# Attention with two heads' scores in the two row halves of TensorE, a pinned order around it, and a readout in two steps

## The chip, the cores and the metric

The kernel runs on one core of one Trainium2 chip. Its engines work in parallel, each through its own list in order: TensorE (PE in the profile; PEld is its weight loads), VectorE (DVE), ScalarE (ACT), GpSimd (POOL) and SyncE (SP, which issues loads). The metric is the device time of one execution in microseconds (us); lower is better. Of several executions the median is taken.

## The reference

Two layers of a hybrid backbone over 512 latent tokens and 256 context tokens of width 1024. Layer 0 is the even mixer: one input projection feeds a gated linear attention (GLA, 4 heads) and a softmax attention with 8 query heads in 2 groups of 64-wide keys and values; both results are concatenated, projected, normalised and added; then a feed-forward layer. Layer 1 is a different recurrence (HGRN2) and another feed-forward layer. What matters here is the attention of layer 0:

```python
def _softmax_attend(q, k, v):
    s = jnp.einsum('bhgqd,bhkd->bhgqk', q, k, preferred_element_type=jnp.float32) * (ATT_HEAD_DIM ** -0.5)
    p = jax.nn.softmax(s, axis=-1).astype(v.dtype)
    return jnp.einsum('bhgqk,bhkd->bhgqd', p, v)
...
    o_lat = jnp.concatenate([a_lat, b_lat], axis=-1)
...
    b_ctx = _softmax_attend(qa[:, :, :, :n_ctx], ka[:, :, :n_ctx], va[:, :, :n_ctx])
```

Latent queries read all 768 keys, context queries only the 256 context keys. The GLA half is read out as `_gated_readout`: a root-mean-square norm of each head times a gate.

## The kernel before

Tokens are handled in six tiles of 128: 0 to 3 latent, 4 and 5 context. Values that need more than one float32r pass are kept as two parts, H (the rounded value) and L (the remainder), and a product is summed from several passes.

**Attention** (class `Attention`). `keys` (L154) transposes keys into `pk` and writes H and L. A head is 64 wide, so each group's keys fill half of the rows; GpSimd copies them into the other half (L165), for both groups. `queries` (L167) transposes a tile's queries; for each head H lies in one half of the rows and L in the other. `scores` (L179) then needs two passes of all 128 rows a head, keys H and keys L, which sum all four products. It fills one `mm` tile (1024 columns, two PSUM banks; there are two such tiles), VectorE takes the row minimum (L196; the keys carry the factor −0.125), ScalarE the Exp with its row sum (L198), VectorE the reciprocal (L199). `turned` (L201) transposes the 768 probabilities in six blocks through two small PSUM tiles and copies them out on ScalarE (the first four) and VectorE (the other two, L210). `values` (L212) multiplies values by transposed probabilities, both groups at once in the two column halves of TensorE, into `po` (attO in the profile). `rows` (L230; rB) spreads the reciprocals, `done` (L248) multiplies them on (L252) and splits the result into H and L of `cat`, the input of the output projection (L665, L666).

`context` (L255) does tiles 4 and 5, four heads to a tile of scores; `latent` (L304) does tiles 0 to 3 one head a step, 32 heads in all: scores of head i, transposes of head i − 3, a part of the values of the four heads before that. PSUM has eight banks: two `mm` tiles of two, `sc0` and `sc1` of one, two `tr` of one.

**What sets the order.** `even_mixer` (L1068) holds generators under short names and runs them by hand-written lists: `x` is a step of the context's attention, `y` of the latent attention, `r1` a tile of the GLA readout (`readout`, L1174: square, sum, rstd, then two multiplies, L1180 to L1186), `t` a piece of `gated_T` (L1270; transposes of the GLA output into `cat`, catT), `M` a step of `mod_group` (L507; loads of eight 512 KB blocks, then 32 small matmuls, then two transposes), `g1` a part of the GLA gates. After the first `y x y g1` the list is

```python
            run("x y x y M x y x")
            behind = {6: "t", 7: "r1", 9: "t", 10: "r1", 14: "M", 15: "r1", 16: "M", 17: "t", 19: "t", 22: "t", 24: "t", 26: "t", 29: "t"}
            for i in range(3, 32 + 7):
                run("y " + behind.get(i, ""))
```

While `self.pinned` is set, `mm` and `tr` (L370, L373) keep all matmuls and transposes in the order in which the program issues them. Instructions of ScalarE and VectorE are not pinned: the scheduler of the framework orders them by its own estimate of when they can start. What follows, `out_proj` (L1523), is not pinned either, so that its matmuls can move forward between those of attention. It loads eight units of 128 rows of `even_w_out`; `unit` (L688) loads a block on SP into one of three `raw` tiles and splits it into H on ScalarE (L699) and L on VectorE (L700).

Of the kernel before, what the change touches and what calls it, by code (L numbers as in the profile page):

```python
# [133 lines left out]
class Attention:  # L134
# [10 lines left out]
    def __init__(self, net, natq, natk, cat):  # L145
        self.net, self.nc, self.natq, self.natk, self.cat = net, net.nc, natq, natk, cat
        self.q, self.k, self.po, self.r, self.o, self.ended = {}, {}, {}, {}, {}, []

    def other(self):

        t = list(self.po)[-1]
        return t % 2 if t in self.ended else 1 - t % 2

    def keys(self, g, gn, HL):  # L154

        nc, net, half = self.nc, self.net, self.half
        pk = net.tr_tile("kT")[:, : gn * P]
        for i in range(gn):
            net.tr(pk[:, i * P : (i + 1) * P], self.natk[:, g + i, 0:128], net.ident)
        for n in range(2):  # L160
            H, L = (x[half[n], n, :] for x in HL)
            nc.scalar.mul(H, pk[half[n]], -0.125)
            nc.vector.scalar_tensor_tensor(L, pk[half[n]], -0.125, H.bitcast(F32), op0=ALU.mult, op1=ALU.subtract)
            for x in HL:
                nc.gpsimd.tensor_copy(x[half[1 - n], n, :], x[half[n], n, :].bitcast(F32))  # L165

    def queries(self, t, q):  # L167
        nc, net, half = self.nc, self.net, self.half
# [4 lines left out]
        for n in range(2):  # L173
            H = q[half[n], 4 * n : 4 * n + 4, :]
            nc.scalar.copy(H, pv[half[n]])
            nc.vector.tensor_tensor(q[half[1 - n], 4 * n : 4 * n + 4, :], pv[half[n]], H.bitcast(F32), op=ALU.subtract)
        self.q[t] = q

    def scores(self, t, heads, p):  # L179

        nc, net = self.nc, self.net
        s = net.mm_tile("S")
        nk = p.shape[-1]
        w = 1024 // len(heads)
        for x, hd in enumerate(heads):
            at = w * x
            for ks in self.k[int(t >= LT)]:
                m = ks[0].shape[-1]
                for i, k in enumerate(ks):
                    net.mm(s[:, at : at + m], self.q[t][:, hd, :], k[:, hd // 4, :], start=(i == 0), stop=(i == 1))  # L190
                at += m
        sv = s.rearrange("p (x k) -> p x k", k=w)[:, :, :nk]
        mx, sm = (net.sm.tile([P, len(heads)], F32, tag=tag, name=tag) for tag in (("amx", "asm") if len(heads) == 1 else ("ms4", "ss4")))
        if t not in self.r:
            self.r[t] = net.sm.tile([P, 8], F32, tag="ars", name="ars")
        nc.vector.tensor_reduce(mx, sv, axis=AX.X, op=ALU.min)  # L196
        for x in range(len(heads)):
            nc.scalar.activation(p[:, x, :], sv[:, x, :], AF.Exp, bias=mx[:, x : x + 1], scale=-1.0, accum_out=sm[:, x : x + 1])  # L198
        nc.vector.reciprocal(self.r[t][:, heads[0] : heads[0] + len(heads)], sm)  # L199

    def turned(self, p, dsts, vector, scratch=False):  # L201

        nc, net = self.nc, self.net
        for b, dst in enumerate(dsts):
            m = dst.shape[1]
            pt = net.sc_tile("pT", self.other()) if b and scratch else net.tr_tile("pT")
# [3 lines left out]
            (nc.vector.tensor_copy if b in vector else nc.scalar.copy)(dst, src)  # L210
# [19 lines left out]
    def rows(self, t):  # L230
# [14 lines left out]
        nc.scalar.copy(w[:, :512], pr)  # L245
        self.o[t] = w[:, :512], w[:, 512:]

    def done(self, t):  # L248
        nc, net = self.nc, self.net
        self.ended.append(t)  # L250
        rb, o = self.o.pop(t)
        nc.vector.tensor_tensor(o, self.po[t], rb, op=ALU.mult)  # L252
        net.put(self.cat, slice(4, 8), slice(t * P, (t + 1) * P), o.rearrange("p (j i) -> p j i", j=4))

    def context(self):  # L255
        wp = self.net.wp
        wide = lambda tag, name, dt=F32R: wp.tile([P, WU], dt, tag=tag, bufs=4, name=name)
        kc = wide("wH", "kc").rearrange("p (x n i) -> p x n i", x=2, n=2)
        self.k[1] = [(kc[:, 0], kc[:, 1])]
        ps, pTs = {}, {}  # L260

        def queries(t, tag):
            self.queries(t, wide(tag, f"qs{t}").rearrange("p (h i) -> p h i", h=8))

        def scores(b):
            ps[b] = wp.tile([P, WU], F32, tag="raw", bufs=3, name=f"prob{b}")
            self.scores(LT + b // 2, range(4 * (b % 2), 4 * (b % 2) + 4), ps[b].rearrange("p (x k) -> p x k", x=4))
# [6 lines left out]
        def values(t):  # L274
            self.rows(LT + t)
            self.values(LT + t, 0, lambda n, ci: pTs[2 * t + n][:, :, ci, :])
# [27 lines left out]
    def latent(self, ap):  # L304
        kl = [ap.tile([P, 2, SEQ], F32R, name=f"k{x}") for x in "HL"]
        self.k[0] = [kl] + self.k[1]
        q = lambda t: ap.tile([P, 8, P], F32R, tag="qs", bufs=2, name=f"qs{t}")
# [5 lines left out]
        ahead = 3  # L313
        heads = (0, 4, 1, 5, 2, 6, 3, 7)
        ps, pTs = {}, {}
        for i in range(8 * LT + ahead + 4):
            t, at = divmod(i, 8)
            if t < LT:
                ps[i] = ap.tile([P, NT], F32, tag="prob", bufs=4, name="prob")
                self.scores(t, (heads[at],), ps[i][:, None, :])  # L320
            j = i - ahead
            if 0 <= j < 8 * LT:
                if j % 4 == 0:
                    pTs[j // 4] = ap.tile([P, 2, NTT, 2, P], F32, tag="probT", bufs=2, name="probT")
                to = pTs[j // 4][:, j % 2, :, j % 4 // 2, :]
                self.turned(ps.pop(j), (to[:, :4], to[:, 4:]), (1,), True)
            if 4 <= j:
                t0, x = divmod(j // 4 - 1, 2)
                pT = pTs[j // 4 - 1]
                self.values(t0, 2 * x, lambda n, ci: pT[:, n, ci], (slice(0, 1), slice(1, 3), slice(3, 4), slice(4, 6))[j % 4])  # L330
                if x and j % 4 == 2:
                    self.rows(t0)
                if x and j % 4 == 3:
                    self.done(t0)
            if t + 1 < LT and at == 4:
                self.queries(t + 1, q(t + 1))
# [3 lines left out]
class Net:  # L340
# [3 lines left out]
    def __init__(self, ctx, tc, I, out):  # L344
        self.tc, self.nc, self.I, self.out = tc, tc.nc, I, out
        tc.nc.scalar.preload_act_table_set("silu_and_others")
        self.side = 0
        self.whole = False
# [339 lines left out]
    def unit(self, src, k, n, pool=None, to=None):  # L688
# [10 lines left out]
        nc.scalar.copy(H[:, :m], raw[:, :m])  # L699
        nc.vector.tensor_tensor(L[:, :m], raw[:, :m], H[:, :m].bitcast(F32), op=ALU.subtract)  # L700
        return H[:, :m].rearrange("p (k n) -> p k n", k=k), L[:, :m].rearrange("p (k n) -> p k n", k=k)
# [189 lines left out]
    def rows_unit(self, w, c, pool=None, paired=False):  # L891
# [5 lines left out]
        return self.unit(src, 1, D, pool)  # L897
# [170 lines left out]
    def even_mixer(self, h, mix, zu, last):  # L1068
# [105 lines left out]
        def readout(c, tiles=tiles):  # L1174

            for t0 in tiles:
# [3 lines left out]
                nc.scalar.activation(sq.rearrange("p (t n) -> p t n", t=2), gv[:, t0 : t0 + 2, cs], AF.Square)  # L1180
                ss = self.sm.tile([P, 4], F32, tag="ss4", name="ss4")
                nc.vector.tensor_reduce(ss, sq.rearrange("p (x v) -> p x v", v=P), axis=AX.X, op=ALU.add)
                rs = self.rstd(ss, P, 4, 4.0 if c else 1.0)
                rb = rs.rearrange("p (t h) -> p t h", t=2)[:, :, :, None].to_broadcast([P, 2, 2, P])
# [706 lines left out]
```

## Time and profile before

| | |
|---|---|
| median of three runs | 1740.32 us |
| lowest, highest | 1738.23, 1741.54 us |
| the profiled execution's own time | 1738.56 us |
| its span, first to last instruction | 1736.4 us |
| granted TensorE clock, mean | 0.996 |
| latent attention, first scores to last values | 259.9 to 354.0 us of the span |

The span is the part of an execution that the profile covers. Lines L... are lines of the kernel's file; since all matmuls go through two helpers, TensorE's rows are told apart by the tiles: S is scores, pT transposed probabilities, attO values, rB reciprocals, qT and kT query and key transposes, catT the GLA output, mod_acc the modulation. A row such as `out<-in engine op shape x6` merges neighbours of one kind. Matmuls are pipelined, so a row's length holds its latency too; the pace is read from starts. What stands in brackets is idle time of the engine ahead of the row and who ended it; "issue" means nobody that the profile shows. Where a float32 matmul (not float32r) is one instruction in the program, the trace has two.

### The profile page before, as it was taken

How to read it: one execution, taken by the hardware profiler on the slowest of the kernel's cores; microseconds unless marked ns; L12 is line 12 of the kernel's file. 1: busy time of each engine (PE TensorE's matmuls, PEld its weight loads, DVE VectorE, ACT ScalarE, POOL GpSimd, SP SyncE). 2: the span in 40 equal slices, each digit the busy share in tenths (PEclk: the TensorE clock that was granted, in tenths of full speed). 3: DMA queues.
4: the chain of work that ended last, by engine and by line, in shares of the span. 5: the costliest groups of instructions: out<-in, count | busy, mean ns of one | idle time of the engine just before them, and what ended most of it. 6: DMA issues, size and time to landing. Idle time of an engine off the chain costs nothing. (4 is left out here: it accounts for less than half of the span.)

```text
span 1736.4 us, 31825 instructions
## 1 busy us (share of the span) xinstructions
PE 1691.2 (97%) x13252; PEld 1516.2 (87%) x13252; DVE 1280.1 (74%) x2036; ACT 857.3 (49%) x1467; POOL 75.7 (4%) x93
## 2 busy tenths in 40 slices
PE   6999999999999999999999999999999999999998
PEld 3989986778999999989997889999988889999997
DVE  5879658735966979886668658787865678778785
ACT  5545557736543333333347436665644754444342
POOL 1004100001000000000001000000000000000000
PEclk8999999999999999999999999999999999999999
DMA  8631013154332424332234762121124333333333
GB/s 320 214 121 39 2 36 105 34 157 146 107 100 73 145 86 138 105 122 69 66 97 170 259 186 64 39 62 50 44 68 146 110 109 101 95 99 108 96 99 122
DMA packets 165548, 187.18 MB, mean 108 GB/s; under 512 B 6262, under 2 KB 132764, under 8 KB 165404
## 3 DMA queue, kind: packets, MB, share of 16 engines
q1 hardware_dynamic: 163472, 181.56, 33.2%
q10 hardware_dynamic: 1932, 3.59, 0.6%
q8 instruction: 104, 1.70, 0.4%
q14 instruction: 40, 0.33, 0.1%
HBM read 175.66 MB, written 9.46 MB: 107 GB/s over the span
## 5 line engine op out<-in xcount | busy, mean ns | idle before, releaser
L764 ACT CAST wH<-raw 128x1024 fp32r<-128x1024 f32 x120 | 124.8, 1052 | 197.7 <-DVE y L857 78.4
L371 PE MATMUL nat<-wH,x 128*128 128x256 f32 (+2 forms) x944 | 214.7, 319 | 0.0
L700 DVE TENSOR_TENSOR wL<-raw,wH 128x1024 fp32r<-128x1024 f32 (+1 forms) x126 | 151.3, 1207 | 59.4 <-ACT wH L699 58.3
L765 DVE TENSOR_TENSOR wL<-raw,wH 128x1024 fp32r<-128x1024 f32 x120 | 145.3, 1222 | 66.2 <-ACT wH L764 66.0
L699 ACT CAST wH<-raw 128x1024 fp32r<-128x1024 f32 (+1 forms) x126 | 129.0, 1041 | 107.8 <-PE nat L371 31.9
L371 PE MATMUL acc<-wH,gH 128*128 128x512 f32 x440 | 171.8, 390 | 0.0
L371 PE MATMUL acc<-wH,gL 128*128 128x512 f32 x440 | 171.5, 390 | 0.0
L371 PE MATMUL acc<-wL,gH 128*128 128x512 f32 x440 | 171.5, 390 | 0.0
L371 PEld LDWEIGHTS nat<-wH,x 128*128 128x128 f32 x944 | 158.2, 191 | 13.6 <-issue 0.8
L371 PE MATMUL nat<-wL,x 128*128 128x256 f32 (+2 forms) x472 | 149.0, 316 | 0.0
L857 DVE TENSOR_TENSOR y<-y,acc 128x1024 f32<-128x1024 f32 x135 | 115.1, 863 | 36.9 <-PE acc L371 32.9
L371 PE MATMUL ff<-x,wH 128*128 128x384 f32 x512 | 132.1, 339 | 0.0
L554 DVE SCALAR_TENSOR_TENSOR macc<-mraw,scT,macc 128x1024 f32<-128x1024 f32 x98 | 122.9, 1281 | 7.5 <-DMA mraw<-in_mod_w_dram 7.3
L624 POOL TENSOR_TENSOR rs<-ms,neghalf 128x1 f32<-128x1 f32 (+2 forms) x62 | 59.3, 957 | 1537.7 <-DVE ms L622 1537.5
L371 PE MATMUL oproj<-wH,x 128*128 128x512 f32 x320 | 101.9, 395 | 0.7 <-ACT x L1281 0.7
L371 PEld LDWEIGHTS acc<-wH,gL 128*128 128x128 f32 x440 | 82.6, 188 | 17.3
L371 PEld LDWEIGHTS acc<-wH,gH 128*128 128x128 f32 x440 | 82.7, 188 | 16.6
L371 PEld LDWEIGHTS acc<-wL,gH 128*128 128x128 f32 x440 | 82.7, 188 | 16.4
L371 PEld LDWEIGHTS nat<-wL,x 128*128 128x128 f32 x472 | 90.3, 191 | 5.0
L371 PEld LDWEIGHTS ff<-x,wH 128*128 128x128 f32 x512 | 91.3, 188 | 0.4
L965 ACT COPY qkh<-arr 128x512 f32<-128x512 f32 x112 | 70.3, 642 | 37.9 <-DVE arr L970 31.8
L371 PE MATMUL ff<-x,wL 128*128 128x384 f32 x256 | 85.6, 335 | 0.0
(345 smaller groups left out, 4028.0 us busy)
## 6 DMA issues: line engine op xcount, KB each, us to landing
mraw<-in_mod_w_dram SPq DMA_DIRECT2D x96, 512.0 KB, 4.5
raw<-in_ffn_w_gate_dram SPq DMA_DIRECT2D x44, 512.0 KB, 3.7
raw<-in_ffn_w_up_dram SPq DMA_DIRECT2D x44, 512.0 KB, 4.0
raw<-in_ffn_w_down_dram SPq DMA_DIRECT2D x44, 512.0 KB, 3.6
raw<-in_odd_w_in_dram SPq DMA_DIRECT2D x40, 512.0 KB, 3.8
raw<-in_even_w_in_dram SPq DMA_DIRECT2D x16, 512.0 KB, 4.5
x<-xr SPq DMA_DIRECT2D x14, 512.0 KB, 2.6
xr<-x SPq DMA_DIRECT2D x14, 512.0 KB, 7.8
```

What stands on the lines that cost most here:

```text
L371: return self.pin(self.nc.tensor.matmul(*a, **k))
L554: nc.vector.scalar_tensor_tensor(a, u, w, a, op0=ALU.mult, op1=ALU.add)
L624: nc.gpsimd.tensor_tensor(rs, ms, self.neghalf.to_broadcast([P, w]), op=ALU.pow)
L699: nc.scalar.copy(H[:, :m], raw[:, :m])
L700: nc.vector.tensor_tensor(L[:, :m], raw[:, :m], H[:, :m].bitcast(F32), op=ALU.subtract)
L764: self.nc.scalar.copy(H, f)
L765: self.nc.vector.tensor_tensor(L, f, H.bitcast(F32), op=ALU.subtract)
L857: nc.vector.tensor_tensor(y, y, pt, op=ALU.add)
L965: nc.scalar.copy(qkv[:, :, :, half, :], dst)
```

## The change

- **Scores.** Keys and queries are kept as H and L for both groups, one group in each half of the rows; the copies to the other half go. A step takes two heads, head m of either group. It issues three passes (H by H, H by L, L by H), each as two matmuls of 64 rows, one in each row half, into two different score tiles. The fourth product, L by L, is left out. A step so takes both `mm` tiles.
- **Step.** 16 steps (and three more to drain) instead of 32 heads. A step issues the scores, the 12 transposes of the step before in three banks of four (`turned_bank`; bank 0 and 2 copied out by ScalarE, bank 1 by VectorE), both minima, both Exps; then, behind a `yield`, rows, half of the values of an earlier pair of steps, the last copy, the reciprocals, `done`, the next queries. Copy of bank 0 is issued ahead of the Exps, that of bank 2 behind the values.
- **Context.** A tile of scores holds two heads of either group, by the same three passes.
- **Order.** Work of ScalarE and VectorE in attention, `gated_T` and the second readout goes through `pin`, so it too keeps the program's order. `readout` yields between the norm and the two multiplies. New lists place the other work; `inner` stands between the two halves of a step.
- **Units ahead.** A new kind `u` loads three units of `even_w_out` and splits them during attention; `out_proj` takes them as ready.

```diff
     def keys(self, g, gn, HL):
...
-        for n in range(2):
-            H, L = (x[half[n], n, :] for x in HL)
-            nc.scalar.mul(H, pk[half[n]], -0.125)
-            nc.vector.scalar_tensor_tensor(L, pk[half[n]], -0.125, H.bitcast(F32), op0=ALU.mult, op1=ALU.subtract)
-            for x in HL:
-                nc.gpsimd.tensor_copy(x[half[1 - n], n, :], x[half[n], n, :].bitcast(F32))
+        H, L = HL
+        net.pin(nc.scalar.mul(H, pk, -0.125))
+        net.pin(nc.vector.scalar_tensor_tensor(L, pk, -0.125, H.bitcast(F32), op0=ALU.mult, op1=ALU.subtract))
...
+    def scores(self, t, ms):
+        net, half = self.net, self.half
+        if t < LT:
+            ss = [net.mm_tile("S") for _ in range(2)]
+        else:
+            s = net.mm_tile("S")
+            ss = [s[:, 512 * n : 512 * n + 512] for n in range(2)]
+        at = 0
+        for m in ms:
+            for k in self.k[int(t >= LT)]:
+                size = k[0].shape[-1]
+                for i, (a, b) in enumerate(((0, 0), (0, 1), (1, 0))):
+                    for n in range(2):
+                        net.mm(
+                            ss[n][:, at : at + size], self.q[t][half[n], a, m, :], k[b][half[n]],
+                            start=(i == 0), stop=(i == 2), tile_position=(64 * n, 0),
+                        )
+                at += size
...
+    def turned_bank(self, b, ps, dst, side):
+        nc, net = self.nc, self.net
+        pt = net.sc_tile("pT", side) if b == 2 else net.tr_tile("pT")
+        for i in range(4):
+            n, c = divmod(4 * b + i, NTT)
+            net.tr(pt[:, i * P : (i + 1) * P], ps[n][:, c * P : (c + 1) * P], net.ident)
+        src = pt.rearrange("p (c i) -> p c i", c=4)
+        return lambda: net.pin((nc.vector.tensor_copy if b == 1 else nc.scalar.copy)(dst[:, 4 * b : 4 * b + 4, :], src))
...
+        for s in range(4 * LT + 3):
+            t, m = divmod(s, 4)
+            copies, sums = [], []
             if t < LT:
+                ss = self.scores(t, (m,))
+            if 1 <= s <= 4 * LT:
...
+                copies = [self.turned_bank(x, old, dst, 1 - (s - 3) // 4 % 2) for x in range(3)]
+                copies.pop(0)()
+            if t < LT:
...
+                exps = [self.softmax(x[:, None, :NT], p[:, None, :]) for x, p in zip(ss, ps[s])]
+                sums = [(self.r[t][:, 4 * n + m : 4 * n + m + 1], x()) for n, x in enumerate(exps)]
+            if copies:
+                copies.pop(0)()
+            yield
+            if s >= 5 and s % 4 == 1:
+                self.rows(s // 4 - 1)
+            if 3 <= s:
...
+                self.values(t0, 2 * x, lambda n, ci: pTs[b][:, n, ci], (slice(0, 3), slice(3, 6))[late])
+            if copies:
+                copies.pop(0)()
+            for r, sm in sums:
+                net.pin(self.nc.vector.reciprocal(r, sm))
+            if s >= 6 and s % 4 == 2:
+                self.done(s // 4 - 1)
+            if m == 0 and 0 < t + 1 < LT:
                 self.queries(t + 1, q(t + 1))
             yield
...
+        def ahead():
+            for c in range(3):
+                split = self.rows_unit(I["even_w_out"][0], c, later=True)
+                yield
+                self.ready.append(split())
...
+            run("y x y g1 x y x y r1 M x y x y r1")
+            inner = {3: "t", 7: "t", 11: "t", 15: "t"}
+            behind = {2: "r1", 3: "t", 5: "r1", 6: "M", 7: "t", 8: "M r1", 9: "r1 u", 11: "t", 13: "u", 15: "t", 16: "u", 17: "u"}
+            for i in range(2, 4 * LT + 3):
+                run("y " + inner.get(i, "") + " y " + behind.get(i, ""))
...
     def out_proj(self, wop, pp, w, cat, tiles, end, paired):
...
+        ready, self.ready = self.ready, []
+        units = [ready[c] if c < len(ready) else self.rows_unit(w, c) if c < 4 else self.rows_unit(w, c, wop, paired) for c in range(KD)]
```

153 lines of the change are left out of this document (70 added, 83 removed).

## The prediction

> **What bounds the kernel now.** The page comes first, for the engine that fills the span.
>
> ```profile
> span 1736.4 us, 31825 instructions
> PE 1691.2 (97%) x13252; PEld 1516.2 (87%) x13252; DVE 1280.1 (74%) x2036; ACT 857.3 (49%) x1467; POOL 75.7 (4%) x93
> ```
>
> A mean of 97% says nothing of one stage, so the second view is the table by windows, cut where the character of attention changes: from the first latent scores to the end of the context's work, the even rows of heads, the tail, and the output projection behind it. Columns: window, its length, busy time of PE, PEld, DVE, ACT, POOL with instruction counts, granted clock, DMA share, GB/s.
>
> ```profile
> 259.90:276.10 16.20, 13.49 (x93) 9.94 (x91) 13.99 (x26) 12.64 (x25) 1.01 (x1) 1.00 0.71 245
> 276.10:342.30 66.20, 66.10 (x531) 47.05 (x529) 51.24 (x107) 49.82 (x93) 2.02 (x2) 1.00 0.12 33
> 342.30:354.00 11.70, 11.70 (x99) 7.92 (x97) 5.35 (x12) 6.06 (x11) 0.00 (x0) 1.00 0.44 136
> 354.00:433.00 79.00, 77.39 (x370) 64.65 (x369) 37.53 (x51) 42.27 (x84) 7.84 (x12) 1.00 0.44 143
> ```
>
> From 276.1 us to the end of attention TensorE does not stop (66.10 of 66.20 us), and behind it hardly (77.39 of 79.00). There, TensorE time saved is time won, and nothing else is. Only the first 16 us have stops, about 2.7 us. The waits of that window name them: transposes wait for VectorE to empty their buffer, scores for an Exp.
>
> ```profile
> PEld pT L374 <- DVE probT L210: 2.5, 3, 1.3
> PEld S L371 <- ACT prob L198: 2.0, 3, 0.8
> ```
>
> [...]
>
> ```profile
> 285.94 0.19 PEld L371 LDWEIGHTS S<-kH,qs 128*128 128x128 f32 x1 [0.39 <-issue]
> 286.05 0.19 PEld L371 LDWEIGHTS S<-kL,qs 128*128 128x128 f32 x1
> 286.28 0.42 PEld L371 LDWEIGHTS S<-kc,qs 128*128 128x128 f32 x2
> 286.64 0.68 PEld L374 LDWEIGHTS pT<-ident,prob 128*128 128x128 f32 x6
> 287.49 0.20 PEld L371 LDWEIGHTS attO<-probT,natk 128*64 128x64 f32 x4 [0.17 <-issue]
> 288.07 0.19 PEld L371 LDWEIGHTS S<-kH,qs 128*128 128x128 f32 x1 [0.39 <-ACT probT L210]
> ...
> 290.64 0.20 PEld L374 LDWEIGHTS qT<-ident,natq 128*128 128x128 f32 x2 [0.39 <-ACT probT L210]
> ```
>
> Scores take 286.64 − 285.94 = 0.70 us: two streams of 512 columns at 0.23 (286.05 to 286.28) and two of 256 at 0.12. Six transposes and the step to the next form take 0.85 (286.64 to 287.49), the values of one chunk of keys 0.58 (287.49 to 288.07), together 2.13. The next head, to 290.64, takes 2.57, since every other head has two chunks: 0.44 more. Two heads are 290.64 − 285.94 = **4.70 us**, without the work that is put between heads.
>
> **Scores in the row halves.** Two heads need 2 × 2 full-height passes now, and then three passes of two half-height matmuls (the low-by-low product falls away). If the halves run side by side, that is 3 × 0.23 + 3 × 0.12 = 1.05 us for 1.40. The trace has such pairs already: the GLA readout multiplies 64-row operands of two heads in turn.
>
> ```profile
> 245.01 1.86 PEld L371 LDWEIGHTS pog<-Sg,arrg 64*128 64x128 f32 x32
> 247.00 1.01 PEld L371 LDWEIGHTS S<-kc,qs 128*128 128x128 f32 x8
> ```
>
> 32 half-height ones of 128 columns take 247.00 − 245.01 = 1.99 us, 0.06 each, where a transpose, as wide and full-height, takes about 0.11 (0.65 of the 0.85 above, over six). So halves do run side by side. That was float32, and scores are float32r, which stream twice as fast; no row has a half-height pair at that pace. The bounds are 1.05 us (side by side; less is excluded, for each half streams all its columns) and 2.10 (one after the other); I take 1.05, as the nearest row behaves.
>
> If a pair takes what a transpose takes, 16 of them are 1.75 to 1.8 of the 1.99 us; the other 0.20 is the change of form, and the same is left of 0.85 over six transposes. Changes of form number two a head now (transposes to values, values to scores), four for two heads; then three (scores to transposes is new). Per pair: scores 1.05 + 0.20, transposes 12 × 0.109 + 0.20 = 1.51, values 3 × 0.44 + 0.14 = 1.46, together **4.2 us for 4.7**. [...]
>
> **What the pair of tiles costs.** Both halves end together and hold both of the two S buffers, so the next scores wait until the second Exp is through. The trace has each link:
>
> ```profile
> 261.78 0.95 DVE L196 TENSOR_REDUCE amx<-S 128x1 f32<-128x768 f32 x1
> ...
> 262.77 0.90 ACT L198 ACTIVATE prob<-S,amx 128x768 f32<-128x768 f32 x1 [0.46 <-DVE amx L196]
> ...
> 263.57 0.19 ACT L198 ACTIVATION_READ_ACCUMULATOR prob<-S,amx 128x1 f32 x1
> 263.81 0.19 PEld L371 LDWEIGHTS S<-kH,qs 128*128 128x128 f32 x1 [0.74 <-ACT prob L198]
> ```
>
> Reduce to Exp is 0.99 (261.78 to 262.77), Exp to the next scores 1.04 (to 263.81). With the scores' own 1.05, some 0.30 until VectorE sees the last of them (the S row below) and the second reduce's 0.95 that makes 4.33 us a step, 0.13 over TensorE's 4.20. All TensorE work of the next step is queued behind the waiting scores. But rows, query and cat transposes (four are 0.44) and the modulation's sums lie between the scores of 10 of the 13 steps from step 3 on, and fill 0.13. So from step 3 TensorE should still set the pace.
>
> **The start.** Steps 0 to 2 have no latent values to fill with. I walk them with these rows, first of TensorE, then of the groups by line (the last figure ahead of the second bar is the mean in ns):
>
> ```profile
> 259.89 0.19 PEld L371 LDWEIGHTS S<-kH,qs 128*128 128x128 f32 x1
> ...
> 264.70 0.85 PEld L371 LDWEIGHTS rB<-ident,ars 128*64 128x64 f32 x16
> 265.52 0.25 PEld L371 LDWEIGHTS attO<-probT,natk 128*64 128x64 f32 x4
> ...
> 267.44 0.19 PEld L371 LDWEIGHTS S<-kH,qs 128*128 128x128 f32 x1 [0.81 <-ACT prob L198]
> ...
> 273.16 0.19 PEld L371 LDWEIGHTS S<-kH,qs 128*128 128x128 f32 x1 [0.44 <-ACT prob L198]
> ```
>
> ```profile
> L210 ACT COPY probT<-pT 128x512 f32<-128x512 f32 x34 | 19.8, 584 | 12.0 <-PE pT L374 11.9
> ...
> L371 PE MATMUL S<-kc,qs 128*128 128x256 f32 x64 | 12.8, 281 | 0.0
> ...
> L700 DVE TENSOR_TENSOR wL<-raw,wH 128x1024 fp32r<-128x1024 f32 x4 | 4.9, 1220 | 1.3 <-ACT wH L699 1.3
> ...
> L666 DVE TENSOR_TENSOR x<-o,x 128x512 fp32r<-128x512 f32 x6 | 4.1, 688 | 4.6 <-ACT x L665 4.6
> L699 ACT CAST wH<-raw 128x1024 fp32r<-128x1024 f32 x4 | 4.1, 1043 | 0.9 <-PE mod_acc L371 0.9
> ...
> L665 ACT CAST x<-o 128x512 fp32r<-128x512 f32 x6 | 3.7, 620 | 5.4 <-PE nat L371 3.4 <-DVE o L252 2.0
> ...
> L252 DVE TENSOR_TENSOR o<-attO,o 128x512 f32<-128x512 f32 x5 | 3.4, 690 | 5.1 <-PE attO L371 5.1
> ...
> L1185 DVE TENSOR_TENSOR gvo<-gvo,rs 128x512 f32<-128x512 f32 x3 | 2.1, 690 | 1.9 <-POOL rs L624 1.9
> ```
>
> Step 0: the query transposes wait for a buffer that ScalarE empties, now pinned behind both Exps: 1.35 + 0.99 + 0.90 + 0.99 + 0.58 = 4.8, and 0.6 for the transposes gives 5.4. Step 1 is full of TensorE work: scores 1.25, transposes 1.5, rB 0.82, context values 1.92 (265.52 to 267.44): 5.5. Step 2: VectorE holds, in pinned order, the context's product, a wait for its cast on ScalarE, its remainder and the readout's two multiplies ahead of the first reduce: 0.69 + 0.62 + 0.69 + 2 × 0.69 = 3.4; then the two reduces, the second Exp and the wait, 0.95 + 0.99 + 1.04, in all 6.4. So 17.3 us to step 3, where six heads took 273.16 − 259.89 = 13.27 before: **+4.0**, less 0.85 since one head more is transposed by then.
>
> **The sum.** Steps 3 to 15: 13 × 0.50 = −6.5. Cat and query transposes behind the values now return to another form: 6 × 0.20 = +1.2. In step 13 the early weight split, 1.04 on ScalarE behind the step's Exps and copies and then 1.22 on VectorE, holds the next reduce by an estimated 1.1, and the bare chain shows once for 0.3: +1.4. At the end the last pair's transposes wait for its Exps, 0 to 1.9, since free projection matmuls can fill in: +1.0. Ahead of step 0 the keys lose their GpSimd copies and half of their instructions, and this stop goes:
>
> ```profile
> 227.38 0.30 PE L374 MATMUL qT<-ident,natq 128*128 128x128 f32 x1 [1.10 <-DVE kc L163]
> ```
>
> That is −0.9. The context's scores gain 4 × 0.35 and lose two changes of form each, 4 × 0.40: +0.2. In all 4.0 − 0.85 − 6.5 + 1.2 + 1.4 + 1.0 − 0.9 + 0.2 = **−0.5 us**. Three bank copies a pair for four, fewer query casts, and the loads issued early on SP, behind the modulation's, lie under a TensorE that is full either side, and count nothing; so do the ready units, for the projection never stops. If that cover fails, each late copy shows its 0.58.
>
> The profiled execution took 1738.56 us (2.2 beside its span), 1.8 under the median; on the median's scale the forecast is 1740.3 − 0.5 = **1739.8 us**. What measurement can tell from no change is about 0.2%, 3.5 us.
>
> **The rivals.** *TensorE keeps full throughout.* If VectorE and ScalarE clear their work ahead of the scores in steps 0 to 2 too, the start gives no +4.0 and the later waits (1.4, 1.0) go: 1739.8 − 6.4 = 1733.4. For it: ScalarE and VectorE are busy only 49.82 and 51.24 of 66.20 us. Against it: the pinned order puts late work ahead of reduces. Chance 0.34.
>
> *The chain sets every step.* If pinned VectorE work (done, cat, splits) reaches past the next scores, each step waits 0.4 us more: 13 × 0.4 = 5.2, 1745. It decides once a step's VectorE list is later than 1.35 us behind the next scores' start. Chance 0.12. [...]
>
> *TensorE stands long enough to lose its clock.* Step 2 leaves it idle for up to 6.4 − 1.25 − 1.5 = 3.65 us. At the kernel's start a sparse 3.4 us was followed by 10.2 us at half clock:
>
> ```profile
> 26.25:29.66 3.41, 1.28 (x16) 0.32 (x16) 3.41 (x11) 3.41 (x8) 0.42 (x1) 1.00 1.05 386
> 29.66:39.90 10.24, 8.40 (x53) 4.00 (x54) 5.15 (x15) 3.98 (x9) 0.00 (x0) 0.50 0.77 261
> ```
>
> At half clock such a stretch loses half its length, 1.7 (3.4 us) to 5.1: with 4, 1744. Chance 0.07. [...]
>
> *The halves run in turn.* Then the edit doesn't do what it says: 16 × 1.05 + 4 × 0.7 = 19.6, 1759. Chance 0.05.
>
> **How the numbers follow.** Forecast 0.42, and it is the case within 0.2%. Faster by more than that is the first rival, 0.34. Slower is the other three, 0.12 + 0.07 + 0.05 = 0.24. The range takes in the first rival less 2.4 (the ends of the tail and of the start), and the second and third with 3 more for the unknown waits: 1731 to 1748; the last rival stays out.
>
> **What would show it.** Right: half-height S pairs at 0.23 us, first to next scores 4.2 to 5.3 us from step 3 on, TensorE stops of 2 to 4 us in steps 0 and 2, the wait of qT for ACT's probT and of S for an Exp late in step 2. Wrong: pairs at 0.46; stops ahead of S in most steps (chain); no stop in steps 0 to 2 (full); a clock under 1.00 there.

## The result and the profile after

The kernel after takes **1749.2 us** in the median of five runs (1745.75 to 1750.2); the kernel before took 1739.91 in the five beside them. The ratio is 1.0054, with a 95% interval of 1.0042 to 1.0065: **9.3 us slower**, where the forecast was 1739.8 and the range ended at 1748. In a second series (run 9 below) the ratio was 1.0056 (1.0044 to 1.0069). The profiled execution is the fastest of the five, 1745.75 us, so its span shows somewhat less of the loss than the median does.

The page of the kernel after has the same busy time of TensorE (1691.2 before) in a span that is 7.6 us longer. So TensorE's work did not grow; its idle time did, and part of its busy time ran at a lower clock (0.993 in the mean for 0.996).

```profile
span 1744.0 us, 31977 instructions
PE 1691.3 (97%) x13348; PEld 1517.1 (87%) x13348; DVE 1273.7 (73%) x2012; ACT 848.5 (49%) x1459; POOL 72.5 (4%) x85
```

Where it lies is told by the table of windows, cut at the same events in both traces: the first query transposes of the context part; the first latent scores; the scores of step 3 (of the seventh head, before); the last step's scores (of head 31); the last attention values; the first transposes of the feed-forward layer behind the output projection; the end. First before, then after. Columns: window, length, busy time of PE, PEld, DVE, ACT and POOL with counts, granted clock, DMA share, GB/s.

```profile
224.40:259.90 35.50, 33.16 (x464) 29.66 (x463) 18.56 (x36) 20.13 (x57) 4.05 (x8) 1.00 0.13 38
259.90:273.16 13.26, 11.58 (x82) 8.44 (x80) 11.14 (x21) 10.16 (x21) 1.01 (x1) 1.00 0.87 299
273.16:339.74 66.58, 65.45 (x523) 46.77 (x523) 52.52 (x109) 50.75 (x96) 2.02 (x2) 1.00 0.12 33
339.74:353.65 13.91, 13.91 (x117) 9.66 (x114) 6.91 (x13) 7.47 (x14) 0.00 (x0) 1.00 0.37 114
353.65:385.83 32.18, 32.18 (x144) 26.34 (x141) 12.97 (x16) 10.48 (x15) 2.22 (x4) 1.00 0.49 147
385.83:1736.40 1350.57, 1327.48 (x9300) 1209.29 (x9298) 1009.72 (x1484) 638.21 (x1034) 32.04 (x41) 1.00 0.34 106
```

```profile
224.90:266.30 41.40, 34.53 (x489) 30.60 (x488) 16.49 (x32) 18.26 (x53) 0.00 (x0) 0.96 0.15 46
266.30:281.90 15.60, 11.19 (x106) 8.78 (x105) 11.93 (x21) 8.98 (x19) 1.01 (x1) 1.00 0.66 218
281.90:345.80 63.90, 63.00 (x573) 46.30 (x573) 44.62 (x86) 43.42 (x89) 2.01 (x2) 0.97 0.05 12
345.80:359.50 13.70, 13.28 (x110) 9.43 (x112) 8.03 (x15) 10.07 (x18) 0.00 (x0) 1.00 0.10 33
359.50:395.60 36.10, 33.46 (x143) 25.58 (x140) 14.82 (x18) 10.84 (x15) 2.21 (x4) 1.00 0.72 202
395.60:1744.00 1348.40, 1327.01 (x9300) 1209.43 (x9298) 1009.63 (x1484) 637.04 (x1034) 33.03 (x41) 1.00 0.34 106
```

Row by row, after less before: context part **+5.9**, latent start +2.3, latent steps −2.7, latent end −0.2, output projection **+3.9**, the rest −2.2. With 0.5 ahead of the first row that is the 7.6 us, but for rounding. The latent attention, on which nearly all of the forecast was spent, comes out 0.6 us shorter. The loss lies ahead of it and behind it. The last row has the same instructions in both; in the traces of the experiments below, which change nothing there, it lies between 1348.3 and 1352.5, so its −2.2 is not read as a gain.

**The context part.** The timeline of ScalarE in the kernel before (engine, line, tiles) has a copy of transposed probabilities ahead of the Exps of the scores just issued:

```profile
238.79 0.59 ACT L210 COPY probT<-pT 128x512 f32<-128x512 f32 x1
239.62 0.47 ACT L198 ACTIVATE prob<-S,ms 128x256 f32<-128x256 f32 x1 [0.24 <-DVE ms L196]
```

In the kernel after the same copy stands behind the four Exps, because that is how the program lists them and both are pinned now; ScalarE idles 0.80 us for the row minimum, which it could have spent on the copy:

```profile
239.06 0.47 ACT L202 ACTIVATE prob<-S,ms 128x256 f32<-128x256 f32 x1 [0.80 <-DVE ms L198]
...
240.88 0.59 ACT L216 COPY probT<-pT 128x512 f32<-128x512 f32 x1
```

VectorE's copy of the other four blocks is late as well: it is pinned behind the reciprocal of the row sums, and that waits for the same four Exps. In the kernel before it ran at 239.53, ahead of the reciprocal.

```profile
241.03 0.18 DVE L289 RECIPROCAL ars<-ss 128x4 f32<-128x4 f32 x1 [2.00 <-ACT prob L202]
241.12 0.66 DVE L216 COPY probT<-pT 128x512 f32<-128x512 f32 x1
```

TensorE, whose list is in the same order, waits for the buffer that ScalarE's copy empties; the next such pair of copies does the same 12 us later. Its timeline in the kernel after:

```profile
238.32 0.66 PE L411 MATMUL pT<-ident,prob 128*128 128x128 f32 x4
241.52 1.77 PE L408 MATMUL pdg<-gvo,kng 128*64 128x128 f32 x22 [2.55 <-ACT probT L216]
...
254.00 0.63 PE L411 MATMUL kT<-ident,natk 128*128 128x128 f32 x4 [2.74 <-ACT probT L216]
```

In the trace of before these instructions follow without such a stop (0.24 us at most). ScalarE keeps the listed order: the copy starts at 240.88, 0.10 behind the start of the last Exp's row sum (240.78, 0.21 us).

The first stop has a tail. Windows of the kernel after, around the first stop and around the stop ahead of latent step 3; the clock is the number ahead of the last two:

```profile
238.50:242.44 3.94, 1.39 (x20) 1.15 (x21) 1.28 (x3) 2.40 (x9) 0.00 (x0) 1.00 0.41 133
242.44:245.86 3.42, 3.42 (x28) 2.87 (x25) 2.80 (x7) 0.00 (x0) 0.00 (x0) 0.50 0.00 0
279.90:283.40 3.50, 1.12 (x7) 0.72 (x9) 2.54 (x5) 2.56 (x6) 0.00 (x0) 1.00 0.04 15
283.40:286.82 3.42, 3.42 (x20) 3.20 (x17) 2.92 (x5) 1.53 (x3) 1.01 (x1) 0.50 0.00 0
```

In both pairs TensorE mostly stood in the first window (busy for 1.39 of 3.94 us and 1.12 of 3.50), and its clock is at 0.50 for the 3.42 us behind it; by that clock these do the work of an estimated 1.71. The loads of the 12 transposes from 284.47 on, in the second of them, take 2.41 us; at full clock, in the step from 321.86 on shown below, 1.29.

**The output projection.** The timeline of TensorE shows stops that the kernel before did not have (32.18 busy of 32.18), on the two instructions that split a unit of weights:

```profile
370.57 0.50 PE L408 MATMUL oproj<-wH,x 128*128 128x512 f32 x1 [0.24 <-ACT wH L739]
371.83 0.50 PE L408 MATMUL oproj<-wL,x 128*128 128x512 f32 x1 [0.76 <-DVE wL L740]
```

There are six such stops between 370 and 379 us. Their brackets add up to 2.6 us; by the starts they cost some 4, since the 19 matmuls from 369.94 to 378.57 take 8.6 us and would take 4.4 at the pace of 0.23 just ahead of them. In the list of the weights' raw tiles (operation, count, durations, first and last start) the splits begin at 341.4 (at 299.1 in the kernel before):

```profile
L739 ACT CAST wH<-raw x8: 1047/1048/1084, 341.4 to 375.9; 128x1024 fp32r<-128x1024 f32 x8
```

**The latent attention** looks as forecast. The timeline of weight loads over one step without other work, from one S to the next:

```profile
321.86 0.19 PEld L408 LDWEIGHTS S<-kH,qs 64*128 64x128 f32 x2 [0.38 <-ACT prob L202]
321.97 0.19 PEld L408 LDWEIGHTS S<-kL,qs 64*128 64x128 f32 x2
322.20 0.19 PEld L408 LDWEIGHTS S<-kH,qs 64*128 64x128 f32 x2
322.43 0.54 PEld L408 LDWEIGHTS S<-kc,qs 64*128 64x128 f32 x6
323.10 1.29 PEld L411 LDWEIGHTS pT<-ident,prob 128*128 128x128 f32 x12
324.56 1.06 PEld L408 LDWEIGHTS attO<-probT,natk 128*64 128x64 f32 x12 [0.17 <-issue]
326.01 0.38 PEld L408 LDWEIGHTS S<-kH,qs 64*128 64x128 f32 x2 [0.39 <-issue]
```

Two half-height matmuls of 512 columns start every 0.23 us (321.97, 322.20, 322.43), so the halves run side by side: a full-height matmul of 512 columns took the same 0.23 in the kernel before (286.28 − 286.05). (A column of float32r takes about half as long as one of float32 in these traces: 0.23 us for 512 against about 0.11 for the 128 of a transpose.) The step is 326.01 − 321.86 = 4.15 us.

### The profile page after: what moved, and what is told of

Read it like the earlier page. It is cut to its first block, busy times and chain, and to the rows that moved or that the text cites. A ratio compares the mean times of both kernels' runs of the same rounds, so it can differ in the third digit from the quotient of the medians.

```text
span 1744.0 us, 31977 instructions
## 1 busy us (share of the span) xinstructions
PE 1691.3 (97%) x13348; PEld 1517.1 (87%) x13348; DVE 1273.7 (73%) x2012; ACT 848.5 (49%) x1459; POOL 72.5 (4%) x85
```

## The experiments

Theory A: three separate losses, namely the pinned place of the context's copies, the late splits of the ready units, and the stop and half clock early in the latent loop. Its rivals: the form of the context scores costs the time (B), the projection takes up whatever is won ahead of it (C), the projection's stops have nothing to do with the units (D), the latent loop needs the pinned order (E). Ratios are to the kernel before on the same chip, with their 95% intervals.

| kernel | ratio | interval | median, before beside it (us) |
|---|---|---|---|
| after | 1.0054 | 1.0042–1.0065 | 1749.2, 1739.91 |
| 1 context order free | 1.0016 | 1.0007–1.0025 | 1745.01, 1741.51 |
| 2 units not ahead | 1.0026 | 1.0017–1.0035 | 1746.24, 1741.51 |
| 3 both | 0.9996 | 0.9987–1.0004 | 1740.98, 1741.51 |
| 4 ACT and DVE free | 0.9984 | 0.9974–0.9993 | 1740.28, 1741.51 |
| 5 before, context pinned | 1.0036 | 1.0024–1.0049 | 1745.75, 1739.08 |
| 6 splits free | 1.0034 | 1.0022–1.0045 | 1745.05, 1739.08 |
| 7 kernel 3 with filler | 0.9988 | 0.9979–0.9997 | 1736.72, 1739.08 |
| 8 kernel 4, values late | 0.9985 | 0.9976–0.9994 | 1736.96, 1739.08 |
| 9 after, again | 1.0056 | 1.0044–1.0069 | 1748.61, 1738.86 |
| 10 kernel 4, again | 0.9993 | 0.9984–1.0002 | 1738.32, 1738.86 |
| 11 kernel 8, again | 0.9989 | 0.9980–0.9997 | 1736.66, 1738.86 |
| 12 kernel 8 with filler | 0.9985 | 0.9976–0.9994 | 1734.62, 1738.86 |

**1. The context's order free.** All context instructions of ScalarE and VectorE go through a helper that pins the latent ones alone:

```diff
+    def hold(self, r, t):
+        return r if t >= LT else self.net.pin(r)
...
-            net.pin((nc.vector.tensor_copy if b in vector else nc.scalar.copy)(dst, src))
+            (nc.vector.tensor_copy if b in vector else nc.scalar.copy)(dst, src)
```

> The context attention's copies, casts, Exps and reductions on ACT and DVE are taken out of the fixed order; the latent loop's stay in it, and no instruction is added or removed. Theory A (three separate losses: the fixed order in the context part, the readiness of the projection's weights, the stop and half clock early in the latent loop): the stop of 2.72 us at 241.5 us and that of 2.91 us at 254.0 us shrink to under 1 us each, and the time falls by 4 to 6 us, to 1743 to 1745. Rival B (the context scores by halves of the rows, not the order, make the section longer): the first latent score still starts 5 to 6 us later than in the kernel before, and the time stays at 1748 to 1750. Rival C (everything is absorbed at the projection, whose weights come late): the latent loop starts 4 to 6 us earlier and the time still stays within 1 us of 1749.

TensorE's list in this part keeps its order. On ScalarE two copies of transposed probabilities come four Exps earlier; on VectorE the other two come ahead of the reciprocal that waits for these Exps (the first at 238.93). The ratio falls from 1.0054 to 1.0016, about 6.6 us. The timeline of ScalarE and the windows of this kernel (context part, latent start):

```profile
238.30 0.59 ACT L216 COPY probT<-pT 128x512 f32<-128x512 f32 x1
```

```profile
224.80:259.80 35.00, 33.09 (x488) 29.32 (x487) 16.30 (x32) 18.26 (x53) 0.00 (x0) 1.00 0.18 53
259.80:277.42 17.62, 13.27 (x105) 10.40 (x104) 12.01 (x21) 8.96 (x19) 1.01 (x1) 0.90 0.56 197
```

The context part takes 35.00 us, 6.4 under the kernel after and 0.5 under the kernel before. So B falls: with the new form of the scores kept, the part is no longer than before once the copies stand where they stood. In this trace 2.0 us of the gain are lost again in the latent start (17.62 for 15.60, with the clock at 0.90) and 1.5 in the projection (37.61 for 36.10, with the clock at 0.95). Still the median falls, so C falls too.

**2 and 3. The units back at the head of the projection**, alone and together with 1:

```diff
-            behind = {..., 9: "r1 u", 11: "t", 13: "u", 15: "t", 16: "u", 17: "u"}
+            behind = {..., 9: "r1", 11: "t", 15: "t"}
```

> The three weight units that are loaded and split inside the latent loop go back to the head of the output projection, as in the kernel before; all else is the kernel after. Theory A: the splits no longer hold the three raw buffers until the last steps, the loads of the later units start some 12 us earlier, the stops of 0.4 to 0.9 us in the projection go, and the time falls by 3 to 4 us, to 1745 to 1746. Rival D (the projection stops because the attention's last steps end late, whatever the units do): the stops stay, and the time is 1748 to 1750.

> Both edits together: the context part's ACT and DVE work out of the fixed order, and the three units back at the head of the projection. Theory A (the losses add): 7 to 10 us less than the kernel after, 1739 to 1742, so level with the kernel before. Rivals B or D: 1745 to 1750, with the stops in place.

Alone it gives 4.9 us (1.0054 to 1.0026), together 10.1 (to 0.9996), so the two losses all but add (6.6 and 4.9 would be 11.5), and the change without them is level with the kernel before. The windows of kernel 2, context part and projection:

```profile
225.60:271.05 45.45, 38.58 (x488) 33.60 (x486) 16.51 (x32) 18.23 (x53) 0.00 (x0) 0.85 0.14 42
366.05:397.56 31.51, 31.51 (x142) 25.79 (x139) 12.97 (x16) 10.33 (x14) 2.21 (x4) 1.00 0.50 150
```

The projection has no stop and takes 31.51 us, so D falls. The first row is a warning: the context part has the order of the kernel after, unchanged, and took 45.45 where that took 41.40, at a mean clock of 0.85. The same stops cost more or less, by what the clock does after them.

**4. ScalarE and VectorE free throughout**, as in the kernel before; pinned are matmuls and transposes only.

```diff
-    def pin(self, r):
-
-        if self.pinned:
+    pin = lambda self, r: r
+    def hold(self, r):
+        if self.pinned:
...
-        return self.pin(self.nc.tensor.matmul(*a, **k))
+        return self.hold(self.nc.tensor.matmul(*a, **k))
```

> Only TensorE's instructions keep the fixed order; all that the kernel after fixed on ACT and DVE (context, latent loop, readout, unit splits, the gated transposes) is free, as it was in the kernel before. Theory A: the context stops and the late units go together, 1739 to 1743; inside the latent loop little changes. Rival E (the latent loop needs the fixed order, since its Exps and copies otherwise come in an order that TensorE does not expect): the loop's steps 3 to 15 grow from about 5.0 us to 5.5 us and more, and the time is above 1745.

1740.28, 12 us under the kernel after by the ratios. Of rival E one half shows: from step 3 to step 15 the loop takes 67.18 us in this trace and 65.58 in that of the repetition, for 63.90 pinned. The first and the last of these hold 3.4 us at half clock, the second none, so compare 67.18 with 63.90: 3.3 us. About half of that is the splits, which lie early in the loop here (see "What stays open"). But the pinned order gives back far more outside the loop.

**5. The kernel before with the context's Exps and copies pinned**, and nothing else of the change:

```diff
-            (nc.vector.tensor_copy if b in vector else nc.scalar.copy)(dst, src)
+            (lambda r: r if scratch else net.pin(r))((nc.vector.tensor_copy if b in vector else nc.scalar.copy)(dst, src))
...
-            nc.scalar.activation(...)
+            (net.pin if t >= LT else (lambda r: r))(nc.scalar.activation(...))
```

> The kernel before, with one thing of the change alone: the context part's Exps and its copies of the turned probabilities are put into the fixed order, so that two ACT copies fall behind the four Exps of the scores issued just before them; scores, heads, readout and units stay as they were. Theory A (the order of those two copies costs the 5 to 7 us of the context part, whatever the form of the scores): two stops of TensorE near 2.5 to 3 us appear at about 241 and 254 us, the clock drops to half after one of them, and the time is 1746 to 1749 where the kernel before has 1741.5. Rival B (the order only costs something together with scores by halves of the rows): the stops stay under 1 us and the time within 2 us of the kernel before.

1.0036, or 6.3 us by the ratio and 6.7 by the medians, with full-height scores and the old loop. VectorE's copies are late here too (241.81, behind a reciprocal). Its first stop and its context part (35.50 before); with half clock behind both stops, this trace loses 8.0 us here, more than the 6.7 of the medians:

```profile
242.21 1.51 PE L371 MATMUL pdg<-gvo,kng 128*64 128x128 f32 x16 [2.59 <-ACT probT L210]
```

```profile
224.60:268.10 43.50, 36.08 (x464) 32.12 (x463) 18.70 (x36) 20.07 (x57) 4.02 (x8) 0.92 0.11 30
```

The order alone makes the loss, in either direction: taken out of the kernel after it goes, put into the kernel before it comes.

**6. Only the splits free**, the loads still ahead:

```diff
-            pin = self.pin if later else lambda x: x
+            pin = lambda x: x
```

> The kernel after with the three units still loaded inside the latent loop, but the two instructions that split each one free on ACT and DVE. Theory A1 (the fixed place of the splits, in the last steps, holds the raw buffers and so delays the later units' loads): the splits move forward to near 300 to 330 us, the later loads come before 350 us, the projection's stops go, and the time is 1745 to 1747, as with the units at the head of the projection. Rival A2 (it is the loads' place in SP's queue, or the split work itself inside the loop, that costs): the time stays at 1749 to 1751.

1745.05, ratio 1.0034: 3.5 us under the kernel after, most of what kernel 2 won. In its list of raw tiles, and in the window of its projection:

```profile
L739 ACT CAST wH<-raw x8: 1034/1048/1057, 305.6 to 370.9; 128x1024 fp32r<-128x1024 f32 x8
```

```profile
360.48:391.98 31.50, 31.50 (x141) 25.77 (x138) 12.96 (x16) 10.32 (x14) 2.21 (x4) 1.00 0.50 150
```

The splits begin at 305.6 for 341.4, empty the raw tiles so much earlier, and the projection's stops are gone (31.50 for 36.10). So it was not the loads that came too soon, but the splits that were pinned too late, and kept the three raw tiles from the units behind them. (The intervals of kernel 2, 1.0026, and of this one, 1.0034, overlap.) In the kernel after SP issues the loads of the last four units from 357.8 us on, in this one from 309 to 366.5.

**7. A filler in step 2** of kernel 3: 24 transposes of the identity, which nobody reads.

```diff
+            if s == 2: fl = net.sc_tile("fill", 1); [net.tr(fl[:, :P], net.ident, net.ident) for _ in range(24)]
```

> The kernel with the context order free and the units at the head of the projection, which measured 1740.98 with TensorE standing 3.09 us ahead of step 3 and the clock at half for one window after it; 24 transposes of the identity that nobody reads are added to step 2's first half, where TensorE stands, and fill nearly all of the stop. Theory F (the stop itself is the chain's, but the half clock behind it adds to the time): step 3 starts at the same time, the clock stays at 1.00 through steps 3 and 4, and the time falls by 1 to 2 us to 1739 to 1740. Rival G (the steps behind the stop are set by the chain, so that half a clock costs nothing): the half clock goes and the time stays within 0.7 us of 1741. If the transposes themselves run into the chain, the time rises by up to 2 us.

Steps 2 and 3 of kernel 3 (first two rows) and of this kernel:

```profile
271.86:277.57 5.71, 2.79 (x27) 2.29 (x25) 4.81 (x9) 2.67 (x6) 0.00 (x0) 1.00 0.56 184
277.57:285.00 7.43, 7.04 (x42) 5.37 (x42) 4.35 (x11) 5.04 (x11) 1.01 (x1) 0.77 0.01 2
```

```profile
270.59:276.30 5.71, 5.40 (x50) 4.89 (x48) 4.80 (x9) 2.66 (x6) 0.00 (x0) 1.00 0.54 184
276.30:282.16 5.86, 5.47 (x43) 3.89 (x44) 3.74 (x8) 4.57 (x11) 1.01 (x1) 1.00 0.01 3
```

Step 2 takes 5.71 us in both, so the stop is the chain's, from scores through minimum and Exp to the next scores. Step 3 takes 5.86 for 7.43: with TensorE busy through the stop (5.40 of 5.71 us for 2.79) the clock is at 1.00 in step 3, for 0.77, and 1.57 us are won. That is theory F in the trace. Six traces have this stop of 2.9 us without a filler (the two of the kernel after, and kernels 1, 2, 3 and 6), and in all six the clock drops to 0.50 in it or behind it, for 3.4 us (6.8 in kernel 2). The ratios (0.9988 for 0.9996, on two chips) have intervals that overlap, so the time alone does not show it; the mean granted clock over all executions agrees with it (0.9945 beside 0.9950 of the kernel before, and 0.9926 beside 0.9941 without the filler).

**8, 10 and 11. The last context piece moved to step 2** of kernel 4, with both kernels run again on one chip, beside the kernel after (9):

```diff
-            run("y x y g1 x y x y r1 M x y x y r1")
-            inner = {3: "t", 7: "t", 11: "t", 15: "t"}
+            run("y x y g1 x y x y r1 M x y y r1")
+            inner = {2: "x", 3: "t", 7: "t", 11: "t", 15: "t"}
```

> The kernel with ACT and DVE free, which measured 1740.28, and one more edit: the last piece of the context part (the rows of reciprocals and 16 context products, 2.65 us of TensorE at 269 to 272 us) is moved from the second half of step 1 into step 2, where the loop has no products of its own and TensorE stands 1.67 and 1.04 us. Theory F (step 2 to 3 stands for want of independent work): step 2 starts up to 2.6 us earlier, the stop ahead of step 3 shrinks below 1 us, one half-clock window goes, and the time falls by 2 to 4 us to 1736.5 to 1738.5. Rival H (steps 1 to 3 are set by the chain from scores through Exps to the next scores, and step 1 stands where the piece was taken away): the stop moves to step 1 and the time stays within 1 us.

> The kernel after once more, unchanged, beside the next three kernels on one chip, so that their differences can be read without the step from chip to chip. Every theory: 8 to 11 us over the kernel before, ratio 1.005 to 1.006.

> The kernel with ACT and DVE free once more, beside the kernel after. Theory A: 10 to 13 us under the kernel after, 1 to 3 us under the kernel before.

> The kernel with the last context piece in step 2 once more, beside the kernel without that edit on the same chip. Its trace had the last attention product 2.5 us earlier, its ratio to the kernel before was the same. Theory F (the stop ahead of step 3 was worth its length): 2 to 3 us under the kernel without the edit. Rival H (what is won there is given back before the end): within 1 us of it.

On one chip the medians are 1748.61 (after), 1738.32 (kernel 4) and 1736.66 (with the edit). The last two overlap by their intervals, and the traces say that the loop itself won nothing: from the first latent scores to the last values 96.53 us without the edit and 96.50 with it. Step 2 started 2.8 us earlier (267.99 for 270.77), and 3.4 us of it ran at half clock:

```profile
267.99:276.42 8.43, 7.56 (x56) 5.85 (x56) 3.23 (x8) 5.38 (x11) 0.00 (x0) 0.80 0.00 2
```

That is rival H: what was won there was given back before the end. The clock is not the difference between the two, for the trace without the edit holds 3.4 us at half clock too, in step 1 (from 264.56).

**12. Eight filler transposes** ahead of step 2's scores, on top of 8:

```diff
+            if s == 1: fl = net.sc_tile("fill", 1); [net.tr(fl[:, :P], net.ident, net.ident) for _ in range(8)]
```

> The kernel with the last context piece in step 2, and 8 transposes of the identity, read by nobody, ahead of step 2's scores, where its TensorE stood 0.86 us shortly before a window at half clock. Theory F: the half clock at 269 to 273 us goes and the time falls by 1 to 2 us against the kernel without them. Rival G (the drop does not hang on so short a stop, or costs nothing under the chain): within 0.7 us.

```profile
267.31:274.03 6.72, 5.96 (x58) 4.44 (x57) 2.98 (x8) 4.73 (x11) 0.00 (x0) 1.00 0.00 1
```

The same step takes 6.72 for 8.43, with the clock at 1.00 throughout, and the loop 94.85 for 96.50. The median, 1734.62, is 2.0 under the kernel without filler, though here too the intervals overlap; both traces without the filler (8 and 11) drop to a clock of 0.50 in this step (at 269.6 and 270.8 us). This version beats both kernels: 14 us under the kernel after on this chip, and 0.9985 (0.9976 to 0.9994) of the kernel before. The gain on the kernel before is small, and the filler is work for its own sake.

## Why the prediction was wrong

**The step that failed first** is the one on the context: "The context's scores gain 4 × 0.35 and lose two changes of form each, 4 × 0.40: +0.2." It priced the context's scores by TensorE's time alone, and left out that their ScalarE and VectorE instructions are pinned now. The prediction followed the pinned order closely in the latent steps ("now pinned behind both Exps"), and did not look for the same in the context part, where the diff puts the same pins. Measured: +5.9 us. The rest of that sum was near: with the order freed the context part is 0.5 us shorter than before, where −0.9 + 0.2 = −0.7 was forecast. One of its terms is mis-sized: 4 × 0.35 is the gain of passes over 768 keys, and the context's passes read 256. Eight streams of 0.12 become six pairs of 0.12, a gain of 0.24 a tile, so the sum should have been −0.3. (The working reads the parts of a head from the starts of weight loads. In the kernel before, the load for the first kc stream and the kL stream ahead of it both start at 286.28. That moves each part of a head by one stream and leaves the length of a step as it is.)

**The second is**: "so do the ready units, for the projection never stops." The cover that was named, a TensorE that is full, was taken from the kernel before, and the units are what kept it full there. The splits' own price was put at step 13; that they keep three raw tiles from the next loads was not followed. Measured: +3.9 us in the trace, 4.9 by experiment 2. The sentence behind it, "If that cover fails, each late copy shows its 0.58", names bank copies, not the splits.

**Latent start.** Forecast +4.0, less 0.85 for one head more: +3.15; measured +2.3. Steps 0 and 2, forecast at 5.4 and 6.4, took 4.4 and 5.7, step 1, at 5.5, took 5.5, by the starts of their scores:

```profile
266.29 0.19 PEld L408 LDWEIGHTS S<-kH,qs 64*128 64x128 f32 x2 [0.17 <-issue]
...
270.70 0.19 PEld L408 LDWEIGHTS S<-kH,qs 64*128 64x128 f32 x2 [0.17 <-ACT prob L202]
...
276.18 0.19 PEld L408 LDWEIGHTS S<-kH,qs 64*128 64x128 f32 x2 [0.38 <-ACT prob L202]
...
281.89 0.18 PEld L408 LDWEIGHTS S<-kH,qs 64*128 64x128 f32 x1 [3.16 <-ACT prob L202]
```

**Latent steps.** The pair's 4.2 us for 4.70 is right (4.15). For the 12 intervals from step 3 to step 15 the forecast was −6.0 + 1.2 + 1.4 = −3.4; measured −2.7, with one window at half clock in it (283.40 to 286.82) that costs an estimated 1.7. **The end**: forecast −0.5 + 1.0; measured −0.2. From the first latent scores to the last values the forecast came to +0.25 and the traces show −0.6.

**The rivals.** Loss of the clock was held at 0.07. It happened, behind step 2 as described, and once in the context part, an estimated 1.7 us each. That is too little: the two stretches are of the first trace of the kernel after, with a mean granted clock of 0.993 over the whole span, and the second trace has 0.990. Over all executions of run 9 the mean granted clock is 0.9914, beside 0.9949 of the kernel before; 0.0035 of 1747 us is an estimated 6 us of lost clock, an upper bound, as TensorE does not set the pace everywhere. So the stops bring the loss, and by that estimate a good part of its 9.3 us passes through the clock behind them. Alone the clock does not decide: kernel 3 still drops to half clock twice (at 265.7 and 279.4 us) and is level with the kernel before. A stop shorter than the 3.65 us that the prediction gave step 2 was followed by half clock here: 2.55 us of idle time ahead of 241.52. The chain did not set every step, the halves did not run in turn, and TensorE was not full throughout. No rival put a price on a copy that falls behind other work in a pinned list outside the loop, which is why the range ended 1.2 us short.

**What stays open.** In the first traces of kernels 3 and 4 two windows at half clock remain in the latent start; whether a version without filler keeps its clock was not tried. How the 9.3 us divide between the stops and the clock behind them was not measured, since it differs from one execution to the next. One thing that the traces do settle is what the early splits cost: the latent steps of kernel 6 are 1.6 us longer (65.50 for 63.90): 1.9 in steps 7 and 8 (5.58 and 6.36 for 5.05 and 4.96), less 0.35 in step 14. There a split on VectorE (308.13, 1.22 us) holds the minima back to 309.26, which start at 308.18 in the kernel after, and one on ScalarE (311.20, 1.03 us) stands between the two Exps. Kernels 2 and 3, whose splits lie in the same steps, take as long for them; kernel 1, whose splits stay late, does not (5.04 and 4.96).

## What to carry to other kernels

When a change pins an order, walk every engine's list in every stage that it touches, and ask of each copy that empties a buffer what now stands ahead of it; a pin is an edit with a price, though it adds no instruction. Here each late copy on ScalarE had one on VectorE beside it, so by the rows, though no run tried it, moving ScalarE's alone would have left a stop. Work made ready early is free only if it also lets go early of what it holds, here three load buffers. And where the costs of stages add, compare two traces stage by stage at the same events before explaining any of them: the stage that the change is about need not be the one that moved.

## What the hardware showed besides

The same program and the same stops met the clock differently from one execution to the next. These windows are of the kernel after, first in its first profile and then in its second: the second context stop and the 3.4 us behind it.

```profile
250.60:254.00 3.40, 0.66 (x6) 0.44 (x5) 1.40 (x3) 2.40 (x9) 0.00 (x0) 1.00 0.40 128
254.00:257.40 3.40, 3.40 (x37) 2.42 (x38) 0.86 (x2) 1.18 (x2) 0.00 (x0) 1.00 0.07 27
```

```profile
250.60:254.00 3.40, 1.34 (x17) 1.20 (x19) 0.80 (x3) 2.52 (x9) 0.00 (x0) 0.98 0.50 154
254.00:257.40 3.40, 3.40 (x23) 2.13 (x20) 0.65 (x1) 0.58 (x1) 0.00 (x0) 0.52 0.00 0
```

In the first the clock held at 1.00 behind this stop, though TensorE had been busy for only 0.66 of 3.40 us, and had dropped to 0.50 behind the stop before it, at 242.44; in the second it was the other way round, 0.52 behind this stop and 1.00 behind the one before. Around that earlier stop, from 238.60 to 242.00 us, TensorE was busy for 0.85 of 3.40 us in both traces, so how little it worked does not settle it alone. What does is not shown here.

Each of the four stretches at half clock in these windows and around step 3 lasts 3.4 us, and their starts lie whole multiples of that apart: 242.44 and 283.40 in the first trace 40.96 us, 12 times 3.413, and about 253.8 and 284.6 in the second 30.7 us, 9 times 3.41. It may be that a stop's place on this spacing matters. In the first trace the 3.41 us ahead of 242.44 hold 0.92 us of TensorE work, while the second stop lies across two such stretches, 249.27 to 252.68 and 252.68 to 256.09 us, with 1.99 and 2.08. That is an estimate from one trace, and no run was made to test it.

Filler transposes, which nobody reads, went with a clock that stayed up. In experiment 12 TensorE is busy for 2.63 of the 3.40 us from 265.80 on, around the stop, and the clock is 1.00 behind it; in kernel 8 run again (11) for 1.85 of the 3.41 us from 267.20 on, and the clock is 0.53 in the 3.41 us behind them.
